# A blocked WKV recurrence on one core: the second chunk's state chain ahead of the rounding of k, one rounding of v a slot later, three v loads issued by ScalarE

## The chip, the cores and the metric

The kernel runs on one core of a Trainium2 chip. A core has five engines that run side by side, each in the order of its own list of instructions: TensorE (PE, matrix products), VectorE (DVE), ScalarE (ACT), GpSimd (POOL) and SyncE (SP, which here only issues transfers). DMA engines move data between the chip's memory (HBM) and the on-chip memory (SBUF); matrix products land in PSUM, which has eight banks of 2 KB a partition. The metric is the time of one execution on the device in microseconds (us), the median of three runs.

## The reference: what is computed

For each of 16 batches and each of 256 channels a recurrence runs over 2048 time steps. It keeps a weighted sum of v, a sum of the weights, and their common exponent, and gives the ratio at each step:

```python
for t in range(seq_len):
    ww = u + kk
    qq = np.maximum(pp, ww)
    e1 = np.exp(pp - qq)
    e2 = np.exp(ww - qq)
    output[b, t, :] = (e1 * aa + e2 * vv) / (e1 * bb + e2 + 1e-08)
    ww = pp - w + kk
    qq = np.maximum(ww, kk)
    e1 = np.exp(ww - qq)
    e2 = np.exp(kk - qq)
    aa = e1 * aa + e2 * vv
    bb = e1 * bb + e2
    pp = qq
```

k, v and the output are 16 x 2048 x 256 numbers in f32, 33.55 MB each; w and u are rows of 256.

## The kernel before: tiles, slots and queues

**Tiles.** Time is cut into NST = 16 chunks of 128 steps, each chunk into two halves of 64. A tile is one chunk of four batches: 128 time steps on the partitions, 4 x 256 numbers on the columns, 512 KB in f32. There are NP = 64 tiles; tile n belongs to chunk c = n // 4. One pass of the loops over n is called a slot here. Work on several tiles runs in the same slot: the weights of tile n are made, and the outputs of tile q = n - 10 (LAG = 10) and qp = n - 11 are finished.

**What a slot does**, by function and engine:
- load (L67): SP issues the loads of v of tile n + 5 and k of tile n + 6. v has 5 buffers, so the load of v(n + 5) waits until cast_v(n) has read v(n); k has 6. store (L360): SP, output of tile n - 13.
- round_k (L174): VectorE rounds k of tile n + 2 for TensorE. cast_v (L206): VectorE rounds a v tile to bf16.
- logs (L179): TensorE forms the exponents in PSUM. exps (L199): ScalarE takes their exp into the ring EZR. times_v (L212): VectorE multiplies them by v.
- sums (L231): TensorE sums of tile n - 1 over each half, into columns 0 to 255 of the PSUM bank MISC.
- den (L338), recip (L344): denominators of tile q on TensorE, and their reciprocals on ScalarE as exp(-log), with a small piece of other work in between ("recip").
- num (L352) and mult (L356): numerators of tile qp, in two halves that share the one PSUM bank NUMB. VectorE multiplies the first half by the reciprocals, and only then can TensorE write the second.

**The state between chunks** is worked out in small steps spread over the four slots after a chunk: copy_sums (ScalarE), turn (TensorE, into MISC's columns from 256 on), state_logs (ScalarE), state_frames, state_scan and state_offsets (GpSimd and VectorE), state_weights (ScalarE), state_chain (VectorE, four instructions at L299 to L304), turn_back (TensorE, MISC's upper columns), inject (VectorE copies that result at L326; GpSimd issues four DMAs that write it into EZR) and state_next (GpSimd). A list called plan names, for each chunk, the slot and the place within it where each step goes; s = 4c + 3 is the chunk's last slot. For most chunks this puts turn in slots 4c + 4, state_logs in 4c + 5, state_weights and state_chain in 4c + 6, turn_back and inject in 4c + 7. Chunks 0, 1 and 15 have entries of their own.

**Order.** The wrapper K keeps every engine's instructions in the order in which the code issues them. The waits between engines come from the framework, which puts a wait wherever two engines touch the same buffer, in the order of the program. The loop over slots 0 to 9 has one order, the loop over slots 10 to 63 another, and the slots from 64 on finish the last outputs. In slots 10 to 63 the order before is

```python
den(q); small_work(n, "nums"); exps(n); small_work(n, "act")
mult(qp, NUMB, 0)
small_work(n, "mid")
round_k(n + 2)
# casts of v
num(qp, NUMB, 1)
sums(n - 1)
recip(q, lambda: small_work(n, "recip"))
mult(qp, NUMB, 1)
small_work(n, "scan"); times_v(n); small_work(n, "chain"); logs(n + 1)
```

The casts of v are spread unevenly: in slots with n % 4 = 3 two (n and n + 1), with 0 and 1 one (n + 1), with 2 none.

**At the start** SP issues k0, k1, u, v0, k2, v1, k3, v2, k4, v3, k5, v4; ScalarE issues w and then loads its function table (L113). WUH (L405, ScalarE) and WU (L406, VectorE) need u and w, and the first logs need WU.

Of the kernel before, what the change touches and what calls it, by code (L numbers as in the profile page):

```python
# [15 lines left out]
def kernel(  # L16
# [10 lines left out]
    PE, DVE, SC, POOL, SP = nc.tensor, nc.vector, nc.scalar, nc.gpsimd, nc.sync  # L27
# [6 lines left out]
    NP = 4 * NST  # L34
    RING = 12
    AHEAD = 6
# [17 lines left out]
    def rows_of(x, n):  # L54
        c, p = divmod(n, 4)
        return x[4 * p:4 * p + 4, c * TC:(c + 1) * TC, :].rearrange("n t d -> t n d")

    def load_k(n, queue=SP):
        kr_of[n] = kpool.tile([128, 4, Dm], F32, tag="kr", name="kr")
        K(queue.dma_start(out=kr_of[n], in_=rows_of(k, n)))  # L60

    def load_v(n, queue=SP):
        vr_of[n] = vpool.tile([128, 4, Dm], F32, tag="vr", name="vr")
        K(queue.dma_start(out=vr_of[n], in_=rows_of(v, n)))


    def load(n):  # L67
        if n - 1 < NP:
            load_v(n - 1)
        if n < NP:  # L70
            load_k(n)
# [25 lines left out]
    def load_row(eng, r, g0, x):  # L97
        K(eng.dma_start(out=wuf.rearrange("(j r) d -> r j d", r=16)[r, 2 * g0:8], in_=bass.AP(
            tensor=x.tensor, offset=x.offset, ap=[[0, 8 - 2 * g0], list(x.ap[0])])))
# [6 lines left out]
    load_row(SC, 0, 0, w)  # L106
    load_k(1)
    load_row(SP, 1, 2, u)
    load_v(0)
    for n in range(2, AHEAD):  # L110
        load_k(n)
        load_v(n - 1)
    K(SC.preload_act_table_set("natural_log_exp_and_others"))  # L113
    for q in range(2):
        K(POOL.iota(COf[64 * q:64 * q + 64, :], pattern=[[0, 2], [1, HS]], base=-HS // 2 - q, channel_multiplier=0,
# [55 lines left out]
    def ez(n):  # L171
        return EZR[:, :, n % RING]

    def round_k(n):  # L174
        km = consts.tile([128, 4, Dm], F32R, tag=f"km{n % 2}", name="km") if n < 2 else KM[n - 2]
        K(DVE.tensor_copy(km, kr_of.pop(n)))  # L176
        KM[n] = km

    def logs(n):  # L179
        km = KM[n].rearrange("p (i n) d -> p i (n d)", i=2)  # L180

        def rows(q):
            for i in range(2):
                g = 32 * (2 * q + i)
                K(PE.matmul(half(n, q)[:, i, :], CO[g:g + 32, :],  # L185
                            WU[g:g + 32, :].unsqueeze(1).broadcast_to([32, 2, Dm]), start=True, stop=False,
                            tile_position=(g, 0), skip_group_check=True))

        def steps(q):
            for i in range(2):  # L190
                K(PE.matmul(half(n, q)[:, i, :], (NLE, NLZ)[q], km[:, i, :], start=False, stop=True,  # L191
                            skip_group_check=True))

        rows(0)
        rows(1)
        steps(0)
        steps(1)

    def exps(n):  # L199
        if n < TURNS:  # L200
            for q in range(2):
                K(SC.activation(ez(n)[:, q], half(n, q), ACT.Exp))  # L202
        else:
            K(SC.activation(ez(n)[:, 0:2], PS[:, 0:4, :].rearrange("p (q i) x -> p q i x", q=2), ACT.Exp))  # L204

    def cast_v(n):  # L206
        vb = vbpool.tile([128, 4, Dm], BF16, tag="vb", name="vb")
        vr = vr_of.pop(n)
        K(DVE.tensor_copy(vb, vr))  # L209
        VB[n] = vb  # L210

    def times_v(n):  # L212
        vb = VB.pop(n).rearrange("p (i n) d -> p i (n d)", i=2)
        K(DVE.tensor_mul(ez(n)[:, 2:4], ez(n)[:, 0:2], vb.unsqueeze(1).broadcast_to([128, 2, 2, D])))  # L214
# [16 lines left out]
    def sums(n):  # L231
        c, p = divmod(n, 4)
        t = MISC[:, 0:Dm]
        for o in range(2):
            x = 24 - 16 * o - 2 * p
            for j in range(4):
                q, i = divmod(j, 2)
                K(PE.matmul(t[32 * j:32 * j + 32, :], mats["OH"][:, x:x + 32],  # L238
                            ez(n)[:, 2 * q, i, Dm * o:Dm * o + Dm],
                            start=p == 0 and o == 0, stop=p == 3 and o == 1,  # L240
                            tile_position=(0, 32 * j), skip_group_check=True))
# [96 lines left out]
    def den(n):  # L338
        for m, q in (("L", 0), ("Id", 1)):
            for i in range(2):  # L340
                K(PE.matmul(DENB[:, i, :], mats[m], ez(n)[:, q, i, :], start=q == 0, stop=q == 1,  # L341
                            skip_group_check=True))

    def recip(n, between=lambda: None):  # L344
        rd = rpool.tile([128, 2, D], F32, tag="rd", name="rd")
        for i in (slice(0, 1), slice(1, 2)) if n == NP - 1 else (slice(0, 2),):
            K(SC.activation(rd[:, i, :], DENB[:, i, :], ACT.Ln, scale=RS))  # L347
            between()
            K(SC.activation(rd[:, i, :], rd[:, i, :], ACT.Exp, scale=-1.0))  # L349
        RD[n] = rd  # L350

    def num(n, bank, i):  # L352
        for m, q in (("LN", 2), ("IdN", 3)):
            K(PE.matmul(bank, mats[m], ez(n)[:, q, i, :], start=q == 2, stop=q == 3, skip_group_check=True))  # L354

    def mult(n, bank, i):  # L356
        rd = RD[n]
        K(DVE.tensor_mul(rd[:, i, :], bank, rd[:, i, :]))  # L358

    def store(n):  # L360
        K(SP.dma_start(out=rows_of(out, n), in_=RD.pop(n).rearrange("p i (n d) -> p (i n) d", n=2)))
# [10 lines left out]
    for c in range(NST):  # L372
        s = 4 * c + 3
        plan = [(s + 1, "act" if s + 1 < LAG else "recip", copy_sums), (s + 1, "pe", turn),
                (s + 2, "act", state_logs), (s + 2, "mid", state_frames), (s + 2, "scan", state_scan), (s + 2, "scan", state_offsets),
                (s + 3, "recip", state_weights), (s + 3, "chain", state_chain),
                (s + 4, "nums", turn_back), (s + 4, "mid", inject), (s + 4, "mid", state_next)]
        if c == 0:
            plan = [(s + 1, "act", copy_sums), (s + 1, "pe", turn), (s + 1, "pe", state_logs),
                    (s + 1, "round", state_frames), (s + 1, "round", state_scan), (s + 1, "round", state_offsets),  # L380
                    (s + 2, "act", state_weights), (s + 2, "round", state_chain),
                    (s + 3, "pe", turn_back), (s + 3, "round", inject), (s + 3, "round", state_next)]
        if c == 1:
            plan = [(s + 1, "act", copy_sums), (s + 1, "pe", turn), (s + 2, "act", state_logs),
                    (s + 2, "round", state_frames), (s + 2, "round", state_scan), (s + 2, "round", state_offsets)] + plan[6:]
        if c == NST - 1:
            plan = [(s + 1, "copy", copy_sums), (s + 1, "turn", turn),
                    (s + 1, "post", state_logs), (s + 1, "mid", state_frames), (s + 1, "mid", state_scan), (s + 1, "mid", state_offsets),
                    (s + 2, "post", state_weights), (s + 2, "first", state_chain),
                    (s + 3, "turn", turn_back), (s + 3, "first", inject)]  # L390
        for slot, where, f in plan:
            later.setdefault((slot, where), []).append((f, c))

    def small_work(n, where):
        for f, c in later.pop((n, where), []):
            f(c)
# [34 lines left out]
    for n in range(LAG, NP):  # L431

        q, qp = n - LAG, n - LAG - 1
        load(n + AHEAD)

        if qp >= 2:
            store(qp - 2)
        if qp >= 0:
            num(qp, NUMB, 0)
        den(q)  # L440
        small_work(n, "nums")
        exps(n)
        small_work(n, "act")
        if qp >= 0:
            mult(qp, NUMB, 0)
        small_work(n, "mid")
        if n + 2 < NP:
            round_k(n + 2)

        if n % 4 == 3:  # L450
            cast_v(n)
        if n + 1 < NP:
            if n % 4 != 2:
                cast_v(n + 1)
        else:
            times_v(n)
        if qp >= 0:
            num(qp, NUMB, 1)

        sums(n - 1)  # L460
        recip(q, lambda: small_work(n, "recip"))
        if qp >= 0:
            mult(qp, NUMB, 1)
        small_work(n, "scan")
        if n + 1 < NP:
            times_v(n)
            small_work(n, "chain")
            logs(n + 1)
        else:
            den(q + 1)  # L470
        small_work(n, "pe")
# [60 lines left out]
```

## Time and profile before

| | us |
|---|---|
| median of three runs (292.0 to 293.81) | 292.74 |
| profiled execution, time on the device | 294.04 |
| its span | 292.3 |
| granted TensorE clock, mean | 0.99 |

The span runs from the first to the last instruction; the 1.74 us between it and the device time lie outside. The same profile by kind of work, the costliest groups (time on the engine, and the mean of one):

| what | engine | count | busy us | mean ns |
|---|---|---|---|---|
| exp of a tile, L204 | ScalarE | 54 | 101.1 | 1873 |
| mult of an output half, L358 | VectorE | 108 | 74.5 | 690 |
| times_v, L214 | VectorE | 64 | 78.5 | 1227 |
| round_k, L176 | VectorE | 64 | 44.0 | 688 |
| cast_v, L209 | VectorE | 64 | 43.3 | 693 |
| exp and log of the reciprocals, L349 and L347 | ScalarE | 126 | 131.0 | 1056, 1023 |
| copy in inject, L326 | VectorE | 16 | 4.7 | 291 |
| four instructions of state_chain, L299 to L304 | VectorE | 63 | 18.4 | 214 to 442 |

Three loads and stores of 512 KB go with each slot, on SP's queue: 100.42 MB of the 101.53 MB moved, at a mean of 347 GB/s. In the first 50 us the rate is 340 to 350 GB/s, from 60 to 250 us 365 to 381.

A timeline line gives the start and the duration in us, the engine, the line of the code, the operation, the buffers it writes and reads, and in brackets how long its engine had stood idle before it and what ended that wait. "x2" means that two instructions of a group are shown as one.

### The profile page before, as it was taken

How to read it: one execution, taken by the hardware profiler on the slowest of the kernel's cores; microseconds unless marked ns; L12 is line 12 of the kernel's file. 1: busy time of each engine (PE TensorE's matmuls, PEld its weight loads, DVE VectorE, ACT ScalarE, POOL GpSimd, SP SyncE). 2: the span in 40 equal slices, each digit the busy share in tenths (PEclk: the TensorE clock that was granted, in tenths of full speed). 3: DMA queues.
4: the chain of work that ended last, by engine and by line, in shares of the span. 5: the costliest groups of instructions: out<-in, count | busy, mean ns of one | idle time of the engine just before them, and what ended most of it. 6: DMA issues, size and time to landing. Idle time of an engine off the chain costs nothing. (4 is left out here: it accounts for less than half of the span.)

```text
span 292.3 us, 4981 instructions
## 1 busy us (share of the span) xinstructions
PE 257.5 (88%) x1662; PEld 119.7 (41%) x1694; DVE 261.9 (90%) x453; ACT 258.4 (88%) x253; POOL 113.9 (39%) x212
## 2 busy tenths in 40 slices
PE   6976896998989899998989899998989899998881
PEld 2332442534444354444444354444444354433330
DVE  4698989899999999999999999999999999986853
ACT  2765685999999999999999999999999999999892
POOL 7000434153555535253555535253555535242200
PEclk9999997999999999999999999999999999999998
DMA  5999999999999999999999999999999999974686
GB/s 191 356 348 349 348 332 349 334 365 364 378 375 374 380 375 382 379 378 380 380 377 382 380 380 380 377 371 378 379 378 380 370 375 381 370 247 151 222 284 215
DMA packets 103521, 101.53 MB, mean 347 GB/s; under 512 B 4156, under 2 KB 103496, under 8 KB 103496
## 3 DMA queue, kind: packets, MB, share of 16 engines
q1 hardware_dynamic: 101144, 100.42, 100.7%
q0 software_dynamic: 2048, 0.53, 0.8%
q8 instruction: 13, 0.21, 0.3%
q10 hardware_dynamic: 304, 0.27, 0.3%
q14 instruction: 12, 0.10, 0.1%
HBM read 67.12 MB, written 33.55 MB: 344 GB/s over the span
## 5 line engine op out<-in xcount | busy, mean ns | idle before, releaser
L204 ACT ACTIVATE EZR<-PS 128x2048 bf16<-128x2048 f32 x54 | 101.1, 1873 | 7.6 <-PE PS L191 4.9
L358 DVE TENSOR_TENSOR rd<-PS,rd 128x512 f32<-128x512 f32 (+1 forms) x118 | 86.5, 735 | 13.8 <-PE PS L354 7.9
L214 DVE TENSOR_TENSOR EZR<-EZR,vb 128x2048 bf16<-128x2048 bf16 x64 | 78.5, 1227 | 0.7
L349 ACT ACTIVATE rd<-rd 128x1024 f32<-128x1024 f32 (+1 forms) x65 | 67.8, 1043 | 1.2
L347 ACT ACTIVATE rd<-PS 128x1024 f32<-128x1024 f32 (+1 forms) x65 | 65.6, 1010 | 1.4 <-PE PS L341 1.3
L331 POOL DMA_DIRECT2D EZR<-cb x64 | 40.1, 632 | 61.1 <-DVE cb L326 42.3
L354 PE MATMUL PS<-EZR,LN 128*128 128x512 bf16 x128 | 48.7, 380 | 12.8 <-DVE rd L358 10.0
L191 PE MATMUL PS<-km,NLE 128*128 128x512 f32 x128 | 47.2, 450 | 4.1 <-DVE km L176 4.1
L176 DVE CAST km<-kr 128x1024 fp32r<-128x1024 f32 x64 | 44.0, 688 | 2.3 <-DMA kr<-in_k_dram 2.3
L209 DVE CAST vb<-vr 128x1024 bf16<-128x1024 f32 x64 | 43.3, 693 | 2.7 <-DMA vr<-in_v_dram 2.4
L354 PE MATMUL PS<-EZR,IdN 128*128 128x512 bf16 x114 | 43.1, 378 | 0.0
L191 PE MATMUL PS<-km,NLZ 128*128 128x512 f32 x128 | 40.5, 398 | 0.0
L341 PE MATMUL PS<-EZR,L 128*128 128x512 bf16 x127 | 37.8, 378 | 1.8 <-ACT rd L347 1.8
L341 PE MATMUL PS<-EZR,Id 128*128 128x512 bf16 x114 | 35.0, 379 | 0.1
L269 POOL TENSOR_TENSOR F<-LL,LL 128x32 f32<-128x32 f32 x13 | 9.5, 733 | 62.0 <-ACT LL L260 62.0
L185 PE MATMUL PS<-WU,CO 32*128 32x512 bf16 x256 | 27.3, 388 | 3.1 <-DVE WU L406 1.6
L238 PE MATMUL PS<-EZR,OH 128*32 128x256 bf16 x512 | 26.3, 280 | 2.4 <-issue 0.4
L191 PEld LDWEIGHTS PS<-km,NLE 128*128 128x128 f32 x128 | 19.2, 190 | 19.2 <-issue 12.7
L191 PEld LDWEIGHTS PS<-km,NLZ 128*128 128x128 f32 x128 | 24.3, 190 | 5.7
L202 ACT ACTIVATE EZR<-PS 128x1024 bf16<-128x1024 f32 x20 | 19.4, 1019 | 7.9 <-PE PS L191 7.9
L354 PEld LDWEIGHTS <-IdN 128*128 128x128 bf16 x128 | 12.4, 97 | 26.1 <-issue 23.7
L354 PEld LDWEIGHTS <-LN 128*128 128x128 bf16 x128 | 12.8, 100 | 18.5 <-issue 11.5
(71 smaller groups left out, 204.5 us busy)
## 6 DMA issues: line engine op xcount, KB each, us to landing
kr<-in_k_dram SPq DMA_DIRECT2D x64, 512.0 KB, 8.3
vr<-in_v_dram SPq DMA_DIRECT2D x64, 512.0 KB, 8.2
out_dram<-rd SPq DMA_DIRECT2D x63, 512.0 KB, 8.1
EZR<-cb POOLq DMA_DIRECT2D x64, 8.0 KB, 5.2
out_dram<-rd SPq DMA_DIRECT2D x2, 128.0 KB, 3.1
out_dram<-rd ACTq DMA_DIRECT2D x2, 128.0 KB, 3.3
wuf<-in_w_dram ACTq DMA_DIRECT2D x1, 8.0 KB
wuf<-in_u_dram SPq DMA_DIRECT2D x1, 4.0 KB
```

The costliest lines, as they stand in the source:

```text
L176: K(DVE.tensor_copy(km, kr_of.pop(n)))
L185: K(PE.matmul(half(n, q)[:, i, :], CO[g:g + 32, :], WU[g:g + 32, :].unsqueeze(1).broadcast_to([32, 2, Dm]), start=True, stop=False, tile_p ...
L191: K(PE.matmul(half(n, q)[:, i, :], (NLE, NLZ)[q], km[:, i, :], start=False, stop=True, skip_group_check=True))
L204: K(SC.activation(ez(n)[:, 0:2], PS[:, 0:4, :].rearrange("p (q i) x -> p q i x", q=2), ACT.Exp))
L209: K(DVE.tensor_copy(vb, vr))
L214: K(DVE.tensor_mul(ez(n)[:, 2:4], ez(n)[:, 0:2], vb.unsqueeze(1).broadcast_to([128, 2, 2, D])))
L331: K(POOL.dma_start(out=EZR[r:r + 1, 2 * q, r0:r0 + 4, :, :].rearrange("o p i (b x) -> o (p i b) x", b=4), in_=cb[x:x + 32, :]))
L341: K(PE.matmul(DENB[:, i, :], mats[m], ez(n)[:, q, i, :], start=q == 0, stop=q == 1, skip_group_check=True))
L347: K(SC.activation(rd[:, i, :], DENB[:, i, :], ACT.Ln, scale=RS))
L349: K(SC.activation(rd[:, i, :], rd[:, i, :], ACT.Exp, scale=-1.0))
L354: K(PE.matmul(bank, mats[m], ez(n)[:, q, i, :], start=q == 2, stop=q == 3, skip_group_check=True))
L358: K(DVE.tensor_mul(rd[:, i, :], bank, rd[:, i, :]))
```

## The change

Three things are edited, and one follows from them.

The loads at the start: v0, v1 and v2 are issued by ScalarE, between w and its table load; SP's order becomes k0, k1, u, k2, k3, k4, v3, k5, v4.

The plan of chunk 1: state_chain stands in slot 10 at "mid" rather than at "chain", so ahead of round_k(12) and times_v(10) rather than behind them. For that, the weights that it reads must have been made earlier in the program, and so "mid" now stands behind recip.

The order in slots 10 to 63: num of the second half, sums and recip now stand ahead of "mid", round_k and the casts. "mid" is for every chunk the place of state_frames (slot 4c + 5), inject and state_next (slot 4c + 7).

The casts: v of tiles 4c + 8 is rounded in its own slot rather than in the one before. Slots with n % 4 = 3 have one cast, with 0 two, with 1 one, with 2 none.

```diff
     load_row(SP, 1, 2, u)
-    load_v(0)
+
     for n in range(2, AHEAD):
+        load_v(n - 2, SC if n < 5 else SP)
         load_k(n)
-        load_v(n - 1)
+    load_v(AHEAD - 2)
     K(SC.preload_act_table_set("natural_log_exp_and_others"))
...
         if c == 1:
             plan = [(s + 1, "act", copy_sums), (s + 1, "pe", turn), (s + 2, "act", state_logs),
-                    (s + 2, "round", state_frames), (s + 2, "round", state_scan), (s + 2, "round", state_offsets)] + plan[6:]
+                    (s + 2, "round", state_frames), (s + 2, "round", state_scan), (s + 2, "round", state_offsets),
+                    (s + 3, "recip", state_weights), (s + 3, "mid", state_chain)] + plan[8:]
...
             mult(qp, NUMB, 0)
+        if qp >= 0:
+            num(qp, NUMB, 1)
+
+        sums(n - 1)
+        recip(q, lambda: small_work(n, "recip"))
         small_work(n, "mid")
         if n + 2 < NP:
             round_k(n + 2)
 
-        if n % 4 == 3:
+        if n % 4 in (3, 0):
             cast_v(n)
-        if n + 1 < NP:
-            if n % 4 != 2:
-                cast_v(n + 1)
-        else:
+        if n + 1 == NP:
             times_v(n)
-        if qp >= 0:
-            num(qp, NUMB, 1)
-
-        sums(n - 1)
-        recip(q, lambda: small_work(n, "recip"))
+        elif n % 4 < 2:
+            cast_v(n + 1)
         if qp >= 0:
             mult(qp, NUMB, 1)
```

More of the change, by code (lines that the diff above doesn't have):

```diff
@@ L445 @@
             mult(qp, NUMB, 0)
-        small_work(n, "mid")
-        if n + 2 < NP:
-            round_k(n + 2)
-        if n % 4 == 3:
-            cast_v(n)
-        if n + 1 < NP:
-            if n % 4 != 2:
-                cast_v(n + 1)
-        else:
-            times_v(n)
         if qp >= 0:
@@ L461 @@
         recip(q, lambda: small_work(n, "recip"))
+        small_work(n, "mid")
+        if n + 2 < NP:
+            round_k(n + 2)
+        if n % 4 in (3, 0):
+            cast_v(n)
+        if n + 1 == NP:
+            times_v(n)
+        elif n % 4 < 2:
+            cast_v(n + 1)
         if qp >= 0:
```

## The prediction, made before the changed kernel was run

> **What bounds the kernel now.** I read the page's busy shares first, then the timeline of one chunk of four slots on each engine. The page's first lines leave no single winner:
>
> ```profile
> span 292.3 us, 4981 instructions
> PE 257.5 (88%) x1662; PEld 119.7 (41%) x1694; DVE 261.9 (90%) x453; ACT 258.4 (88%) x253; POOL 113.9 (39%) x212
> ```
>
> Three engines are level, so the order of waits decides. VectorE's timeline over slots 35 to 38 (start, duration, instruction, idle before it), cut to the lines that open a slot and to those that the change moves:
>
> ```profile
> 145.74 0.72 DVE L358 TENSOR_TENSOR rd<-PS,rd 128x512 f32<-128x512 f32 x1
> 146.44 0.29 DVE L326 CAST cb<-PS 128x128 bf16<-128x128 f32 x1
> 146.64 0.69 DVE L176 CAST km<-kr 128x1024 fp32r<-128x1024 f32 x1
> 147.24 1.29 DVE L209 CAST vb<-vr 128x1024 bf16<-128x1024 f32 x2
> 148.45 0.68 DVE L358 TENSOR_TENSOR rd<-PS,rd 128x512 f32<-128x512 f32 x1
> 149.05 1.22 DVE L214 TENSOR_TENSOR EZR<-EZR,vb 128x2048 bf16<-128x2048 bf16 x1
> 150.18 0.68 DVE L358 TENSOR_TENSOR rd<-PS,rd 128x512 f32<-128x512 f32 x1
> ...
> 154.24 0.69 DVE L358 TENSOR_TENSOR rd<-PS,rd 128x512 f32<-128x512 f32 x1 [0.44 <-issue]
> ...
> 158.03 0.68 DVE L358 TENSOR_TENSOR rd<-PS,rd 128x512 f32<-128x512 f32 x1
> ...
> 162.17 0.72 DVE L358 TENSOR_TENSOR rd<-PS,rd 128x512 f32<-128x512 f32 x1
> ```
>
> From first multiplication (L358) to first multiplication the slots take 4.44, 4.06, 3.79 and 4.14 us: 16.43 us a chunk, the same between 63.61 and 80.05. VectorE has no gap in the first slot; in the second it is through after 3.53 us (the last times_v starts 152.58, and the next instruction follows a times_v after 1.13) and then stands 0.53 us, because TensorE must first go through num, sums, logs and turn. ScalarE has about 0.40 us of gaps in the same chunk (0.13 before the exp at 148.93, 0.16 before 151.89, 0.11 before 153.33), so it needs 16.03. The loop "VectorE's instructions, with one TensorE detour in slot 4c+4" is the bound from slot 15 to 63. Before that, to about 47 us, the loads are: SP issues them back to back every 1.45 us or so at 340 to 350 GB/s, and VectorE waits 1.73, 0.38, 0.32, 1.05 and 0.81 us for single tiles.
>
> The move of state_chain bears on the start of slots 11 and 12; TensorE, then ScalarE:
>
> ```profile
> 46.59 0.40 PE L320 MATMUL PS<-Id,CB 128*128 128x128 bf16 x4 [2.08 <-DVE CB L304]
> ```
> ```profile
> 50.99 1.88 ACT L204 ACTIVATE EZR<-PS 128x2048 bf16<-128x2048 f32 x1 [3.52 <-PE PS L191]
> ```
>
> turn_back of chunk 1 holds TensorE for 2.08 us, and exps(12) comes 3.52 us late.
>
> **What the Trainium skill says.** "PSUM — Partial Sum Buffer", section on bank collisions: two engines must be kept apart by semaphores per bank and quadrant, even at different columns of a bank. That bears on MISC: one bank, in which sums writes columns 0 to 255 and inject reads columns from 256 on. The trace agrees. In slot 13 state_logs reads MISC's upper columns, and sums stands behind it in the program:
>
> ```profile
> 56.63 0.37 ACT L260 ACTIVATE LL<-PS 128x128 f32<-128x128 f32 x1
> ```
> ```profile
> 56.55 0.38 PE L354 MATMUL PS<-EZR,IdN 128*128 128x512 bf16 x1
> 57.06 0.40 PE L238 MATMUL PS<-EZR,OH 128*32 128x256 bf16 x8
> ```
>
> sums starts 0.51 us after the num matmul before it, where 0.31 is usual (60.42 to 60.73, 76.87 to 77.18), and 0.06 after the read ends at 57.00. "DMA: Bandwidth & Descriptors", "Issuing engines are not separate DMA queues": loads of SP and ScalarE share the same 16 DMA engines, so a second issuer adds no rate; its section on queues adds that an engine takes turns between them. No run here has two big streams. "TensorE: Matmul & The Clock Gate", "What's actually happening": an idle window halves TensorE's clock. The trace agrees: after the 2.08 us stand the pair of NLE matmuls took 1.22 us, elsewhere 0.73.
>
> **The change part by part.**
>
> *Start.* Three 512 KB loads go from SP to ScalarE, ahead of its table load. SP's first issues took 0.40 to 0.51 us each; three of them put the table load from 2.34 to about 3.8 and its end (1.28 us) to 5.1, still ahead of WUH, which waits for u until 6.28. That wait is the cover; if ScalarE were held as SP was at v2 (3.02 us), WUH would come near 8. v0 now takes turns with k1, and u stands behind k1 on SP: u can come up to one tile (1.45 us) later, I take 1.0; v0 comes earlier and its 1.73 us wait goes. The first exp is then some 1.0 late. The bytes and their rate do not change, and after v2 the same tiles have arrived as before, so the waits for k6 (1.05) and k12 (0.81) absorb the delay. Value 0, ends -0.4 and +1.0.
>
> *Chunk 1's state_chain.* Now ahead of round_k(12) in slot 10. Its weights G end at 42.77 and VectorE is free at 42.83, so nothing new is waited for; its four instructions take 0.13 + 0.32 + 0.26 + 0.24 = 0.95 from issue to issue and fill the 0.81 us in which VectorE waited for k12. CB is ready near 44.0, as den(1) ends, and turn_back's wait goes. Late next: num(0,NUMB,1) waits for VectorE's mult, which moves only from 46.33 to about 45.55. So VectorE gains 0.8; then logs(12) no longer starts slot 12 late. If TensorE still slows down it is 0.3, if not, 1.1. Value -0.8.
>
> *Order within a slot.* num(..,1), sums and recip now stand ahead of "mid", round_k and the casts. On each engine's own list nothing moves but the casts: num and sums are TensorE's, recip ScalarE's, mid VectorE's and POOL's. What turns round is who waits for whom on MISC. In slots 4c+7 inject's copy stood ahead of sums(n-1), which waited for it at no cost; now the copy stands behind sums. sums stands behind num(qp,NUMB,1), and that waits for the first mult of the slot:
>
> ```profile
> 146.51 0.38 PE L354 MATMUL PS<-EZR,LN 128*128 128x512 bf16 x1
> 147.04 0.40 PE L238 MATMUL PS<-EZR,OH 128*32 128x256 bf16 x8
> ```
>
> The mult ends 146.46, num starts 146.51, sums ends 147.44; the copy, at 146.44 today, goes to about 147.49: **a new wait of 1.05 us**. Behind it on VectorE stand round_k(n+2) (needed a slot later), the cast, the second mult (which frees NUMB and lets a store go) and times_v(n). Behind it on POOL are inject's four DMAs (2.58 us at 245.55) and state_next; they land 5.2 us after issue, and den needs them three slots (12 us) on. state_frames (POOL) and state_next only change place in the program, not in their waits.
>
> *The moved cast.* cast_v(4c+8) leaves slot 4c+7 (-0.61, the second of two in 1.21) and enters slot 4c+8 (+0.61), where 0.53 of idle takes it in. SP's v load of that slot now waits for it, with a k load and a store behind it: some 1.9 us after the slot starts. SP's queue holds about 8 us of transfers (8.3 us to landing), so the DMA engines don't run dry; the tiles are needed four slots later. Value 0, up to +0.2 a chunk.
>
> *Sum of a chunk.* Slot 4c+7: 4.44 + 1.05 - 0.61 = 4.88. Next slot: 3.53 + 0.61 = 4.14, just over TensorE's 4.06. The others stay 3.79 and 4.14. Together 16.95, **+0.52**; ScalarE's 16.03 stays below. Between 0.35 (if slot 4c+6's 0.16 us gap before its second mult closes) and 0.75 (SP's upper end). Twelve such chunks run from slot 15 to 63: +6.2 (4.2 to 9.0). Slot 63 has the wait with no cast taken out; its times_v, sums(63), turn and the last den follow one another, and ScalarE's next log has 0.24 us to spare: +1.0 (0.5 to 1.05). In all 0 - 0.8 + 6.2 + 1.0 = **+6.4 us**. This is on a profiled execution of 294.04 us (span 292.3 and 1.74 around it), 1.30 above the median; put on the median of 292.74 it gives **299.1**.
>
> **Rivals.**
>
> *The copy does not wait (faster).* If the copy waits only for its own columns, slot 4c+7 takes 3.83 and VectorE's chunk 15.90; ScalarE's 16.03 becomes the bound: -0.40 x 12 - 0.8 = -5.6, 287.1 us. For it: the columns are disjoint. Against: sums at 57.06. It decides below a wait of 0.53 us (16.43 - 15.90); I reckon 1.05.
>
> *The wait is partly hidden.* If logs(12) comes 2 us earlier, and slots 4c+8 and 4c+6 give back what they stand today (0.53 of it is already spent), some +1 to +3.5 remains: 294 to 296.
>
> *Loads fall behind.* A later v load holds k and the store behind it; if the queue runs dry for 0.2 to 0.5 us a chunk, or the start's 1.0 stays, it is 301 to 305. Against: SP stands idle some 3 us in the chunk from 65.83 to 82.26 (13.4 us of issuing in 16.43).
>
> *The change does nothing of this*, as the loops are bound elsewhere: 292.7.
>
> **How the numbers follow.** The wait as worked out: 0.63, 299.1 with its own range 296.7 to 301.5. Partly hidden 0.13, loads behind 0.12, faster 0.09, nothing 0.03. The range 293.5 to 302.5 leaves out the faster case, the lowest part of the next and the worst of the loads. A change within 1% (289.8 to 295.7) can't be told from none here; below it lies the faster case (0.09), within it "nothing" and most of "partly hidden" (0.11), above it the rest (0.80).
>
> **What would show it.** Ahead of L326 on VectorE about 1.0 us of idle, released by TensorE's L238, in each of 14 slots (13 to 15 us in all); a chunk of about 16.95; the idle before the first mult of slot 4c+9 gone; more gaps on ScalarE; turn_back's 2.08 us gone, and exps(12) near 49 to 50 rather than 50.99. No idle ahead of L326 would break the forecast; with it, a chunk still at 16.4 would say that I have the bound wrong. A first exp later than 10.5 us would put the start in question.

## The result, and the profile after

| | before | after |
|---|---|---|
| median of four runs each | 293.25 us (292.0 to 293.81) | 300.44 us (300.07 to 301.77) |
| ratio, 95% interval | | 1.0259 (1.021 to 1.0308) |
| profiled execution; its span | 294.04; 292.3 | 300.57; 298.6 |

The changed kernel is 2.6% slower; between the two profiled spans lie 6.3 us. The kernel before has four runs here, and its median is 293.25 rather than the 292.74 of its first three. Most line numbers are one higher than before, as the edit adds a line: the copy in inject is now L327, the multiplication L359, sums L239. The first lines of the page of the kernel after:

```profile
span 298.6 us, 5011 instructions
PE 263.3 (88%) x1694; PEld 120.1 (40%) x1694; DVE 260.5 (87%) x453; ACT 260.5 (87%) x253; POOL 107.5 (36%) x212
```

VectorE's busy time fell by 1.4 us while the span grew by 6.3, so what was added on VectorE is standing, not work. VectorE's timeline over the same slots 35 to 38 (start, duration, instruction, idle before it):

```profile
147.32 0.71 DVE L359 TENSOR_TENSOR rd<-PS,rd 128x512 f32<-128x512 f32 x1
149.07 0.29 DVE L327 CAST cb<-PS 128x128 bf16<-128x128 f32 x1 [1.03 <-PE PS L239]
149.27 0.69 DVE L177 CAST km<-kr 128x1024 fp32r<-128x1024 f32 x1
149.87 0.69 DVE L210 CAST vb<-vr 128x1024 bf16<-128x1024 f32 x1
150.47 0.68 DVE L359 TENSOR_TENSOR rd<-PS,rd 128x512 f32<-128x512 f32 x1
...
152.21 0.68 DVE L359 TENSOR_TENSOR rd<-PS,rd 128x512 f32<-128x512 f32 x1
...
153.41 1.29 DVE L210 CAST vb<-vr 128x1024 bf16<-128x1024 f32 x2
...
156.35 0.68 DVE L359 TENSOR_TENSOR rd<-PS,rd 128x512 f32<-128x512 f32 x1
...
160.13 0.68 DVE L359 TENSOR_TENSOR rd<-PS,rd 128x512 f32<-128x512 f32 x1
...
164.27 0.72 DVE L359 TENSOR_TENSOR rd<-PS,rd 128x512 f32<-128x512 f32 x1
```

The copy now stands 1.03 us behind sums. From first multiplication to first multiplication the slots take 4.89, 4.14, 3.78 and 4.14: 16.95 us, where they took 4.44, 4.06, 3.79 and 4.14 before. The moved cast shows as the "x2" of 153.41, and the 0.44 us of idle that stood ahead of the multiplication now at 156.35 is gone. TensorE's timeline says what the copy waited for:

```profile
148.09 0.38 PE L355 MATMUL PS<-EZR,LN 128*128 128x512 bf16 x1
...
148.61 0.40 PE L239 MATMUL PS<-EZR,OH 128*32 128x256 bf16 x8
```

The multiplication ends at 148.03, num starts at 148.09, sums ends at 149.01 and the copy starts at 149.07. The table of VectorE's waits (total us, times, longest) has 14 of these, and before it had none:

```profile
DVE cb L327 <- PE PS L239: 14.4, 14, 1.0
```

Where the chunk-1 chain was moved, TensorE and then ScalarE in slots 11 and 12:

```profile
44.20 0.40 PE L321 MATMUL PS<-Id,CB 128*128 128x128 bf16 x4
46.44 0.38 PE L355 MATMUL PS<-EZR,LN 128*128 128x512 bf16 x1 [1.84 <-DVE rd L359]
```
```profile
48.86 1.88 ACT L205 ACTIVATE EZR<-PS 128x2048 bf16<-128x2048 f32 x1 [1.21 <-PE PS L192]
```

turn_back starts at 44.20 without its 2.08 us. The matmul behind it, num, now stands 1.84 us for VectorE's multiplication, and the exp of tile 12 comes at 48.86 rather than 50.99.

The account by places in the two traces: the first multiplication of slot 15 went from 63.61 to 62.64 (-0.97: the start, the chain and the first of the new waits together, and a slower TensorE in the profile before, on which more below); from there to slot 63, from 260.61 to 265.84, twelve chunks added 6.20; the slots from 63 on added 1.03, and the last store is issued at 293.51 rather than 287.25. Together 6.26.

### The profile page after: what moved, and what is told of

It reads as the page before. It is cut to its first block, busy times and chain, and to the rows that moved or that the text cites. A ratio compares the mean times of both kernels' runs of the same rounds, so it can differ in the third digit from the quotient of the medians.

```text
span 298.6 us, 5011 instructions
## 1 busy us (share of the span) xinstructions
PE 263.3 (88%) x1694; PEld 120.1 (40%) x1694; DVE 260.5 (87%) x453; ACT 260.5 (87%) x253; POOL 107.5 (36%) x212
## 3 DMA queue, kind: packets, MB, share of 16 engines
q10 hardware_dynamic: 1888, 1.84, 2.0%
## 5 line engine op out<-in xcount | busy, mean ns | idle before, releaser
L359 DVE TENSOR_TENSOR rd<-PS,rd 128x512 f32<-128x512 f32 (+1 forms) x118 | 86.1, 732 | 7.3 <-PE PS L355 5.7
L332 POOL DMA_DIRECT2D EZR<-cb x64 | 38.7, 611 | 74.9 <-DVE cb L327 61.7
L355 PE MATMUL PS<-EZR,IdN 128*128 128x512 bf16 x128 | 48.4, 378 | 0.0
L342 PE MATMUL PS<-EZR,Id 128*128 128x512 bf16 x128 | 38.1, 379 | 0.0
L270 POOL TENSOR_TENSOR F<-LL,LL 128x32 f32<-128x32 f32 x13 | 10.6, 819 | 60.8 <-ACT LL L261 60.8
L239 PE MATMUL PS<-EZR,OH 128*32 128x256 bf16 x512 | 26.2, 278 | 0.7 <-DVE EZR L215 0.7
```

The source lines that it names most:

```text
L332: K(POOL.dma_start(out=EZR[r:r + 1, 2 * q, r0:r0 + 4, :, :].rearrange("o p i (b x) -> o (p i b) x", b=4), in_=cb[x:x + 32, :]))
```

## The experiments

Each was timed beside runs of the kernel before on the same chip, whose median was 293.07, 293.03 or 292.97. A "chunk" below is the distance from one inject copy to the next. The theory is that the wait of the copy behind sums makes the kernel slower, and that the moved cast gives back about half of it. The rivals: the new order costs in another way, the loads fall behind, or the start is to blame.

**The order without the wait.** The changed kernel with "mid" put back ahead of num and sums, so that the copy is ahead of sums in the program again. Chunk 1's chain alone keeps its new place behind recip, under another name.

```diff
-                    (s + 3, "recip", state_weights), (s + 3, "mid", state_chain)] + plan[8:]
+                    (s + 3, "recip", state_weights), (s + 3, "behind", state_chain)] + plan[8:]
...
             mult(qp, NUMB, 0)
+        small_work(n, "mid")
...
-        small_work(n, "mid")
+        small_work(n, "behind")
```

> The changed kernel with mid put ahead of the second half of num and of sums again, so that inject's copy stands ahead of sums as before; chunk 1's state_chain keeps its new place behind recip; casts and loads as changed. Theory (the copy waits behind sums): no idle ahead of the copy, slot 4c+7 takes 3.83 us, VectorE's chunk would be 15.90 and ScalarE's 16.03 becomes the bound, so a chunk of 16.0 to 16.1; against the kernel before -0.97 by slot 15 and -0.40 in each of 12 chunks, about 287.5 us. Rival (the moved cast, with the v load that waits for it, costs the time): casts are as changed, so still 299 to 301. Rival (the start costs it): loads are as changed, so still slower than before.

Measured: 291.65 us, ratio 0.9953 (0.9933 to 0.9974). The idle ahead of the copy is gone, and with it all of the loss and 1.4 us more: nothing else in the change costs what the wait costs.

```profile
143.59 0.29 DVE L327 CAST cb<-PS 128x128 bf16<-128x128 f32 x1
```

The eight chunks from slot 15 to 47 take 15.85 to 15.89, but then come 16.52, 16.81, 16.76 and 16.70. So the size was missed by 4 us, and there is something that only the late chunks show. Two experiments further down are about that.

**The order alone, and the cast alone.** Both start from the kernel before: the first takes over only the order in the slot, the second only the distribution of the casts.

```diff
             mult(qp, NUMB, 0)
+        if qp >= 0:
+            num(qp, NUMB, 1)
+
+        sums(n - 1)
+        recip(q, lambda: small_work(n, "recip"))
         small_work(n, "mid")
...
         if qp >= 0:
-            num(qp, NUMB, 1)
-
-        sums(n - 1)
-        recip(q, lambda: small_work(n, "recip"))
-        if qp >= 0:
             mult(qp, NUMB, 1)
```

> The kernel before with only the order changed: the second half of num, sums and recip ahead of mid, round_k and the casts; casts, loads and chunk 1's plan as before. Theory: the wait of 1.05 us comes with no cast taken out of its slot, so slot 4c+7 takes 5.49 us and a chunk 5.49 + 4.06 + 3.79 + 4.14 = 17.48; +1.05 x 12 + 1.0 = +13.6, about 306.5 us. Rival (the moved cast costs the time): about as before, 293. Rival (the start): as before.

```diff
-        if n % 4 == 3:
+        if n % 4 in (3, 0):
             cast_v(n)
-        if n + 1 < NP:
-            if n % 4 != 2:
-                cast_v(n + 1)
-        else:
+        if n + 1 == NP:
             times_v(n)
+        elif n % 4 < 2:
+            cast_v(n + 1)
```

> The kernel before with only the casts changed (v of tiles 4c rounded in its own slot). Theory: slot 4c+7 3.83, next slot 4.14, then 3.79 and 4.14, VectorE 15.90, ScalarE's 16.03 binds: -0.40 x 12 = -4.8, about 288.3 us. Rival (the moved cast, with the v load behind it, costs the time): slower than before, up to 300.

Measured, the order alone: 307.62 us, ratio 1.0507 (1.0479 to 1.0534), chunks of 17.46 to 17.49 (the last, before slot 63, 17.39). Its line in the table of VectorE's waits (total us, times, longest):

```profile
DVE cb L326 <- PE PS L238: 14.4, 14, 1.0
```

14.4 us of new standing and 14.6 us of new time: the wait passes into the end undiminished. The chunk is 1.05 above 16.43. The time is 1.1 above the 306.5 that was expected, about one wait: the expectation counted twelve chunks and slot 63, and the wait stands 14 times. The one left out is that of slot 11, and in this profile the first multiplication of slot 15 comes at 64.65 for 63.61.

Measured, the cast alone: 291.72 us, ratio 0.9956 (0.9938 to 0.9974), with chunks of 15.88 or 15.89 for seven from slot 15 on, and then 16.8, 17.5, 17.12, 16.96 and 16.71, so it missed its size by 3.4 us, as the first experiment did. In the changed kernel the moved cast takes the chunk from 17.48 to 16.95 (0.53), and without the new wait from 16.43 to 15.88 (0.55): the same half microsecond in both.

**Independent work between sums and the copy.** The changed kernel with the copy still behind sums in the program, but other work of VectorE put ahead of it: first round_k and the cast, then round_k alone, so that the wait should vanish, or shrink to what round_k doesn't fill.

```diff
-        small_work(n, "mid")
+        if n % 4 != 3:
+            small_work(n, "mid")
         if n + 2 < NP:
             round_k(n + 2)
...
             cast_v(n)
+        if n % 4 == 3:
+            small_work(n, "mid")
```

> The changed kernel with inject and state_next moved behind round_k and the cast in slots 4c+7; everything else as changed, so the copy still stands behind sums in the program, but 1.20 us of VectorE's own work lies in between. Theory (only the uncovered wait of 1.03 us costs): the idle ahead of the copy goes to nearly nothing, a chunk takes 16.0 to 16.1 and the time is 287 to 288.5 us, as without the wait. Rival (it is the dependence on sums itself, or the later DMAs of inject, or the casts): 297 to 301.

```diff
-        small_work(n, "mid")
+        if n % 4 != 3:
+            small_work(n, "mid")
         if n + 2 < NP:
             round_k(n + 2)
+        if n % 4 == 3:
+            small_work(n, "mid")
```

> The changed kernel with inject and state_next behind round_k only in slots 4c+7, so that 0.60 us of the copy's wait of 1.03 is covered and 0.43 left. Theory: a chunk 16.95 - 0.60 = 16.35, near the memory's 16.4 to 16.5; against the changed kernel -0.55 x 12 and nothing in slot 63 (no round_k there): 293 to 294.5 us, idle ahead of the copy 0.4 us each. Rival (the wait counts as a whole or not at all): 300 or 291.

Measured, covered: 291.71 us, ratio 0.9955 (0.9944 to 0.9966), chunks of 16.15 to 16.17 up to slot 47 and 16.48 to 16.94 after it, so the time is 3 us and more above the 287 to 288.5 expected. Half covered: 295.78 us, ratio 1.0088 (1.0065 to 1.0111), chunks of 16.53 to 16.55 (the last 16.46). VectorE's timeline of the half-covered kernel:

```profile
146.23 0.29 DVE L327 CAST cb<-PS 128x128 bf16<-128x128 f32 x1 [0.43 <-PE PS L239]
```

This is the dose and the response: a wait of 1.03 goes with a chunk of 16.95, one of 0.43 with 16.54, a covered one with 16.16, none in the program with 15.88. Chunks before slot 47 are compared here; what slows the late ones comes next. What is not explained by the wait is that a covered wait still costs 0.28 a chunk, and that the half-covered kernel came out 1.3 us above its expectation (chunk 16.54 for 16.35). In the covered kernel, two casts in the slot after take longer; GpSimd's state_next lies beside them. VectorE and GpSimd:

```profile
148.04 1.54 DVE L210 CAST vb<-vr 128x1024 bf16<-128x1024 f32 x2
```
```profile
147.56 0.73 POOL L314 TENSOR_TENSOR y<-AB,G 128x64 f32<-128x64 f32 x1
148.37 0.65 POOL L315 TENSOR_TENSOR AB<-y,tb 128x64 f32<-128x64 f32 x1
```

In the kernel without the wait the same pair of casts takes 1.29, and the two GpSimd instructions, which fall earlier there, 0.33 and 0.32. Another cast beside GpSimd's state_frames takes 0.77 for 0.68. Together that is 0.25 + 0.09 = 0.34, against the 0.28 to be explained. The half-covered kernel has the same thing. VectorE again:

```profile
149.37 0.80 DVE L177 CAST km<-kr 128x1024 fp32r<-128x1024 f32 x1
...
154.23 0.77 DVE L210 CAST vb<-vr 128x1024 bf16<-128x1024 f32 x1
```

These take 0.68 and 0.69 elsewhere; the first lies beside state_next, the second beside state_frames. That makes 0.20, against the 0.19 between 16.54 and 16.35. The Trainium skill, "SBUF — State Buffer", section "Who interferes with whom", says that VectorE's casts can enter modes in which they and GpSimd share one port pair, and that the one that comes second is blocked. That fits what the covered kernel's trace has, a lengthening on both engines at once. In the half-covered one state_next's own two instructions keep their 0.33 and 0.32. The coincidence is shown; the cause was not tried by itself.

**Why the gain stops after eight chunks.** Without the wait a chunk of 15.88 us moves twelve tiles of 0.524 MB (four of k, of v and of output), which needs 396 GB/s. VectorE, in the first kernel of this section:

```profile
212.07 0.69 DVE L177 CAST km<-kr 128x1024 fp32r<-128x1024 f32 x1 [0.49 <-DMA kr<-in_k_dram]
```

Its waits for k come to 4.2 us in 11 places. Six of them, 1.95 us together, lie in the chunks after slot 47; the other five are over before 42 us, where the kernel before has such waits too (2.3 us in 3 places, none after 44 us). The same kernel with half the stores left out, up to the last tile, should need 330 GB/s:

```diff
-        K(SP.dma_start(out=rows_of(out, n), in_=RD.pop(n).rearrange("p i (n d) -> p (i n) d", n=2)))
+        K(SP.dma_start(out=rows_of(out, n)[:, 0:2, :], in_=RD.pop(n)[:, 0, :].rearrange("p (n d) -> p n d", n=2)))
```

> The first experiment's kernel (mid ahead again, cast, chain and loads as changed) that stores only two of each tile's four batches, until the last tile: half of the output is left out, so a slot moves 2.5 tiles rather than 3. There a chunk took 15.88 us up to about 188 us and 16.5 to 16.8 after that, with waits for k. Theory (the memory rate of some 380 GB/s is the floor that took the expected gain: 12 tiles in 15.88 us are 396 GB/s, and the loads' lead is used up after eight chunks): with 330 GB/s asked for, all chunks take 15.9 us, no waits for k, and the time is 3.3 us less, 288 to 288.5 us. Rival (the late chunks are slow for another reason, such as a wait between engines): 16.5 to 16.8 stay and the time stays at 291 to 292.

Measured: 285.47 us, ratio 0.9736 (0.9718 to 0.9755), all chunks from slot 15 to slot 63 between 15.82 and 15.90. Windows of about a chunk, by engine (stretch; length; busy time of PE, PEld, DVE, ACT and POOL; clock; DMA share; GB/s). First the kernel before, then the one with its "mid" put back, early and late, then that with half the stores:

```profile
130.00:146.43 16.43, 15.29 (x102) 7.21 (x104) 15.84 (x27) 15.97 (x16) 7.57 (x13) 1.00 1.09 380
```
```profile
127.70:143.58 15.88, 15.18 (x102) 7.17 (x104) 15.73 (x27) 15.70 (x16) 6.98 (x13) 1.00 1.09 378
...
207.05:223.57 16.52, 15.04 (x103) 7.09 (x104) 15.85 (x26) 15.55 (x16) 8.15 (x13) 1.00 1.09 379
```
```profile
204.00:220.00 16.00, 15.29 (x104) 7.27 (x106) 15.85 (x27) 15.82 (x16) 6.97 (x13) 1.00 1.02 330
```

The last column is the point. In the kernel with its "mid" put back it stands between 373 and 380 in each of the ten chunks from 64 us on, whether a chunk takes 15.88 or 16.52. At 15.88 the kernel uses 396 and is given 378: by this estimate each chunk eats some 0.7 us of the lead that the loads had, and when that is gone VectorE waits for k. With half the stores 330 is enough, and no late chunk waits. The kernel before, at 6.29 MB in 16.43 us, needed 383: it ran at about this rate already, though no load kept VectorE waiting after 44 us. The time fell further than reckoned. Between the two profiled spans lie 5.3 us (289.0 and 283.7): 3.3 of them are in the four chunks from slot 47 on, which is the part in question (2.0 are idle time of VectorE, nearly all of it the six waits for k, and 1.3 are longer instructions on VectorE, whose cause was not tried); 1.2 lie before slot 15, where runs of kernels with full stores differ by as much among themselves (the copy of slot 15 at 64.16 here, at 62.70 with the cast alone); and 0.8 come after slot 63, where less was waiting to be stored.

**The loads alone, and the chain alone.** The kernel before with the three v loads given to ScalarE; and the kernel before with chunk 1's weights and chain in slot 10 ahead of round_k, with sums(9) and recip(0) ahead of them in that slot alone.

```diff
-    load_v(0)
+
     for n in range(2, AHEAD):
+        load_v(n - 2, SC if n < 5 else SP)
         load_k(n)
-        load_v(n - 1)
+    load_v(AHEAD - 2)
```

> The kernel before with only v0, v1 and v2 issued by ScalarE. Theory: the first exp about 0.9 us later (9.2 to 9.4), taken back by tile waits by slot 6; the time within 0.5 us of before. Rival (the start costs some of the 7 us): +1 or more. Rival (the start gave the 0.45 us by which slot 6 was earlier in the changed kernel, and it lasts): -0.5.

```diff
-                    (s + 2, "round", state_frames), (s + 2, "round", state_scan), (s + 2, "round", state_offsets)] + plan[6:]
+                    (s + 2, "round", state_frames), (s + 2, "round", state_scan), (s + 2, "round", state_offsets),
+                    (s + 3, "recip", state_weights), (s + 3, "behind", state_chain)] + plan[8:]
...
         small_work(n, "mid")
+        if n == LAG:
+            sums(n - 1)
+            recip(q, lambda: small_work(n, "recip"))
+            small_work(n, "behind")
...
-        sums(n - 1)
-        recip(q, lambda: small_work(n, "recip"))
+        if n > LAG:
+            sums(n - 1)
+            recip(q, lambda: small_work(n, "recip"))
```

> The kernel before with only chunk 1's state_chain ahead of round_k(12), for which sums(9) and recip(0) stand ahead of it in slot 10 alone. Theory: turn_back's wait goes, slot 15 comes 0.5 to 1.0 us earlier, chunks stay at 16.43 (12 tiles in it are 383 GB/s, the memory's rate, so part may be given back as waits for k): 292.1 to 293 us. Rival (the stall at turn_back is worth what it shows, 2.1 to 3.5 us): 289.5 to 291.

Measured, the loads: 293.58 us, ratio 1.0014 (1.0001 to 1.0028), so +0.4 us, 0 to 0.8. Measured, the chain: 292.84 us, ratio 0.999 (0.9972 to 1.0009), so -0.3 us, between -0.8 and +0.3: the runs can't tell it from nothing. Its profile has turn_back without its wait, at 43.83, num standing 1.70 us for VectorE's multiplication, and the exp of tile 12 at 48.33. So the mechanism is there, and its worth in time stays open. TensorE's standing has moved rather than gone: 2.08 us at turn_back before, 1.70 at num now.

The profile before also shows something here that is not the chain's. Its TensorE ran at a granted clock of 0.50 from 48 to 50 us, and the exp of tile 12 was 3.52 us late. With the cast alone the same stand of 2.08 us was followed by a clock of 1.00; in the first kernel of this section turn_back waited only 0.25 (and num 1.85), and yet the clock went to 0.56. ScalarE in these two:

```profile
49.34 1.88 ACT L204 ACTIVATE EZR<-PS 128x2048 bf16<-128x2048 f32 x1 [1.89 <-PE PS L191]
```
```profile
50.49 1.88 ACT L205 ACTIVATE EZR<-PS 128x2048 bf16<-128x2048 f32 x1 [2.14 <-PE PS L192]
```

Of the eleven profiles five have the low clock at this place, three with the chain where it was and two with the chain moved; that of the changed kernel has not. From the first multiplication of slot 11 to that of slot 15 the profile before took 17.28 us, the kernel with the chain alone, at the full clock, 16.40.

**The parts that help, together.** The kernel before with the chain and the cast, with inject's place ahead of sums, and without the move of the loads; it is the first kernel of this section less the edit at the start.

```diff
-                    (s + 2, "round", state_frames), (s + 2, "round", state_scan), (s + 2, "round", state_offsets)] + plan[6:]
+                    (s + 2, "round", state_frames), (s + 2, "round", state_scan), (s + 2, "round", state_offsets),
+                    (s + 3, "recip", state_weights), (s + 3, "behind", state_chain)] + plan[8:]
...
         small_work(n, "mid")
-        if n + 2 < NP:
-            round_k(n + 2)
-
-        if n % 4 == 3:
-            cast_v(n)
...
         sums(n - 1)
         recip(q, lambda: small_work(n, "recip"))
+        small_work(n, "behind")
+        if n + 2 < NP:
+            round_k(n + 2)
+
+        if n % 4 in (3, 0):
+            cast_v(n)
...
+        elif n % 4 < 2:
+            cast_v(n + 1)
```

> The kernel before with two parts of the change, the moved cast and chunk 1's state_chain behind recip, and without the two others: mid stays ahead of num's second half and of sums for inject, and SP issues all loads. Theory: chunks of 15.88 us until the loads' lead is gone and 16.5 to 17 after that; the memory's rate sets the end, so no more than the first experiment gave, less the 0.5 us of the loads at the start: 291.0 to 291.7 us. Rival (the gains of cast and chain add up in full): 287 to 288.

Measured: 291.21 us, ratio 0.9942 (0.9921 to 0.9963), with waits for k of 5.6 us in 14 places, 12 of them after 182 us. It has the lowest median of the kernels with the whole output, 0.6% below the kernel before; the intervals of the others near 0.9955 overlap its own.

## Why the prediction was right

**The wait.** Worked out as 1.05 us from the order multiplication, num, sums, copy; measured 1.03, 14 times. Undone, the loss goes; alone, it costs 14.6; halved, it costs about half. The statement that the prediction took from the Trainium skill, "PSUM — Partial Sum Buffer", section on bank collisions, that engines must be kept apart by bank and not by column, is how the waits in this program lie: the copy reads columns 256 and up, sums writes 0 to 255, and the copy starts 0.06 us after sums ends. Nor is it the whole buffer that is guarded: all eight banks are one tile in the code, and in the prediction's lines of slot 13 num writes the bank NUMB from 56.55 while state_logs reads MISC from 56.63. What is shown is where the framework puts a wait and what that costs; whether the chip needs it was not tried.

**The cast.** -0.61 in one slot, and +0.61 with idle time to take in most of it in the next: slots of 4.88, 4.14, 3.79 and 4.14 were forecast, 4.89, 4.14, 3.78 and 4.14 came. Twelve chunks of +0.52 are the 6.20 us from slot 15 to 63. Slot 63 and what follows gave +1.03 for 1.0. What the sum left out is the first chunk: the prediction looks for the wait in 14 slots but adds it up from slot 15 on, and the wait of slot 11 is in no term. If that chunk gained what the later ones did, this is another +0.5, by estimate.

**The chain.** turn_back's wait went, and the next one late was num behind the multiplication, as forecast. Slot 12's exp came at 48.86 rather than in 49 to 50. The -0.8 is at the edge of what the runs allow: by the medians the chain alone is worth -0.3, between -0.8 and +0.3. It was sized on a profile in which TensorE's clock fell after the stand, and the prediction took the one for the effect of the other; the profiles of the experiments have the stand at turn_back without the low clock, and the low clock without that stand.

By the two profiles the whole came to 6.3 for the forecast's 6.4, and that is partly luck: the wait of slot 11 was left out, and the profile before has a low clock that the one after has not. An estimate from the 17.28 and 16.40 above is that this clock cost up to 0.9 us; without it the two profiles would lie about 7.1 apart. The medians lie 7.2 apart. So the median of after came 1.3 above the forecast: 0.8 because the change cost 7.2 rather than 6.4, and 0.5 because the forecast started from 292.74 and not 293.25.

**The start.** Value 0, and it holds within its bounds (+0.4), but not by the steps given. u was to come 1.0 late and came 0.2 late; among the profiles with the old start it differs by 0.15. v0 was to come earlier and its 1.73 us wait to go. Instead, in the timelines of TensorE, VectorE and SP after:

```profile
8.02 1.22 PE L192 MATMUL PS<-km,NLE 128*128 128x512 f32 x2
```
```profile
10.08 0.69 DVE L210 CAST vb<-vr 128x1024 bf16<-128x1024 f32 x1 [2.06 <-DMA vr<-in_v_dram]
```
```profile
10.07 0.37 SPq L64 DMA_DIRECT2D vr<-in_v_dram  x1
```

v0's cast starts 0.53 later than before, with a longer wait. Over all profiles it starts at 8.62 to 9.55 in the five with the old start and at 10.05 to 10.71 in the six with the new one. The first exp is 0.9 late because TensorE ran slowly here (1.22 for a pair that took 0.73 before), not because of the loads: with the loads moved alone that pair takes 0.73, and with the order alone, where SP issues them as before, it takes 1.22 and the first exp comes at 9.23. And SP stood for 3.6 us until v0 had landed before it issued v3, which nothing in the prediction foresaw. As forecast, the waits for tiles that follow absorb this: the exp of slot 6 starts at 26.05 to 27.01 with the old start and at 26.43 to 27.44 with the new one.

**The wait is partly hidden.** Tile 12's exp did come 2.1 us earlier, as this rival supposed, but nothing took in the wait: from slot 15 on every chunk is 16.86 to 16.96, and with the order alone 14.4 us of standing are 14.6 us of time.

**Loads fall behind.** SP's v loads wait more for casts, 53.9 us in 37 places against 17.6 in 15, yet the rate from 70 to 250 us stays at 365 to 381 GB/s and VectorE's waits for k are 1.7 us in all. This rival had no part.

**The rival that was faster** was rightly given little, but its number, 287.1, rested on a wrong floor. It took ScalarE's 16.03 as the bound once VectorE had 15.90. Without the wait the chunk is 15.88, VectorE's own figure, with ScalarE busy for 15.70; and what bounds the kernel in the end is the transfers, which the prediction had called idle for some 3 us a chunk from what SP's issuing showed. SP's queue was idle, the transfers were not. The share of the DMA engines, 1.08 and 1.09 in the windows of that kernel, would not have shown it: with half the stores, where nothing waits, it still reads 1.02. The rate does. The Trainium skill, "HBM Reference", section "Specifications (TRN2)", has about 425 GB/s for a core that streams alone. No slice of the pages of these runs passes 383, so the measured figure is the one to count with. The truth of that rival is -1.4 us, not -5.6.

## What to carry to other kernels

Where two engines use one PSUM bank and the framework guards it as here, the order of the program decides who waits, even for columns that don't touch: keep the short reader ahead of the long chain of matmuls, or put work that doesn't need the bank between them, and price a reordering by the chain that now stands ahead. Before a gain in a compute loop is counted, divide the bytes of an iteration by its new time and compare that with the rate that the profile has actually reached; a lead in the buffers can hide the difference for many iterations, so read the last ones and not the first. And a term of under 1 us should not be sized on a single profile: look first whether its clock, or the arrival of a tile, differs in another profile of the same code.

## What the runs showed of the hardware that was not expected

- Loads and stores together got 373 to 380 GB/s in the chunks that waited for k, and no slice of a page with full stores passes 383. Loads alone got about 348 (340 to 357 in the slices from 7 to 36 us), with SP issuing all of them or ScalarE three.
- VectorE's casts of 128x1024 took 0.77 to 0.81 us rather than 0.69 where GpSimd's two-input operations ran beside them. In the covered kernel these took 0.65 and 0.73 rather than 0.33.
- v0 issued by ScalarE while SP issues k0 and k1 landed 0.5 to 2.1 us later than when SP issued it in fourth place (six profiles against five), and SP's next load of v stood until then.
- TensorE's speed at the start and after a stand differs between profiles in which the code there is the same. The first pair of matmuls took 0.72 to 0.78 us in seven profiles, 0.95 in one and 1.22 in three; after a stand of 2.08 us the clock was 0.50 in one profile and 1.00 in another.
